# The second attention layer of a two-block network and its norm, put at the head of the scheduler's queue

## Chip, cores and metric

One Trainium2 chip, and of it one core. The metric is the time of one execution on the device in microseconds (us), as the median of several runs; lower is better. The profile is of one execution.

## What is computed

A first block of two layers works on 256 tokens of width 1024; a second block follows it. In the first block each layer is a norm, an attention with two families of heads, an output projection, a second norm and a gated feed-forward with a short causal convolution:

```python
for i in range(DEPTH):                       # DEPTH = 2, S = 256, D = 1024
    h = rms_norm(x, ln_attn_g[i])
    dq, dk, dv, mq, mk, mv = jnp.split(h @ w_in[i], cuts, axis=-1)   # 6 x 512 columns
    ...                                      # heads of dq, dk, mq, mk are normed
    y_diff = diff_attention(dq, dk, dv, lam, lam_init, diff_subln_g[i], bias_diff)
    y_moba = moba_attention(mq, mk, mv, bias_moba)
    x = x + jnp.concatenate([y_diff, y_moba], axis=-1) @ w_out[i]
    x = x + conv_ffn(rms_norm(x, ln_ffn_g[i]), w_up[i], conv_w[i], conv_b[i], w_down[i])
```

The second block takes this x (the "latent") and a second sequence of 256 tokens (the "context"). Its first layer runs a recurrence (rwkv7) over both, forwards and backwards: the context's end states are the start states of the latent's. The context's half of that needs nothing of the first block.

## The kernel before

Every product of activations and weights is made of three matrix products: `weights` (L256 to L270) loads a block of weights into a tile `raw` by a DMA on SP, rounds it into `whi` on ACT (L265), and puts the difference `raw - whi` into `wlo` on DVE or GpSimd (L269); `proj` (L276) and `feat_block` (L298) then issue three matmuls for each 128 rows. TensorE (PE) thus has dense stretches of matmuls wherever weights flow.

Three lanes of work share the engines, each with its own pools of tiles: the latent (`self.lat`), the context (`self.cx`) and a side lane (`self.sd`) with a few small tiles. The kernel is written in the order first norm, setup, `context1` (the context's part of the second block's first layer, with its recurrence in two groups of head pairs), first layer 0, feed-forward 0, `rest` (the modulation `ada` of layer 0), norm 1, first layer 1, `side` (`ada` of layer 1, and the tables of `setup_odd`), feed-forward 1, second block. No order is written out by hand: a list scheduler plays the program through with planned durations and, on each engine, takes among the instructions that are ready the one that was written first. What comes out is a fixed order on each engine's queue; on the chip each queue runs in that order. Tiles of one tag are given out in the order in which they are written, so an instruction that needs a tile waits for the tiles of that tag that are written ahead of it.

By that rule all of `context1` stands ahead of first layer 1 wherever both are ready, and `side` and feed-forward 1 stand behind it. In the profile first layer 1 runs from about 531 to 745 us: its norm (`norm_T`, L354, with `rstd`, L334), six projections of 512 columns (`prj`, L292 to L294), each of them but the two of values followed by a norm of heads (`head_norm`, L385: squares on ACT, sums L394 and some ten small operations on DVE, and the product `hn` at L401), transposes (`q_T`, `k_T`), four heads of `diff_att`, `diff_out` (L618, another `head_norm`), four pairs of `moba_att`, and the output projection `wo`. A projection holds two of the four PSUM banks of tag A until its `hn` is written. The context's lines are those of `rwkv_group` (from L1155 on: `low`, `kss`, `rsq`, `AR`, `BK`, `sc`, `G`, `bkt`, the solve on GpSimd at L1333 and L1335, and the chain of eight steps, L1363 to L1433); the matmuls of `ada` are L778. Feed-forward 1 is `g`, `up` and `acc`. After its last matmul the scheduler may issue the context's output projection (`co`, in `context2`).

What the change touches:

```python
        net.rest()
        act1=net.first_norm(1, x)
        net.first_layer(1, x, act1)
        net.side()
        net.conv_ffn(1, x)
```

Of the kernel before, what the change touches and what calls it, by code (L numbers as in the profile page):

```python
# [1762 lines left out]
def run(tc, I, out, colw, cstw, keep):  # L1763
    nc = tc.nc
    with ExitStack() as ctx:
        net = Net(tc, I)
        net.pools(ctx)
        net.setup(colw, cstw, keep)
        x = [net.keep([128, D], F32, name=f"x{t}") for t in range(2)]
        for t in range(2):  # L1770
            nc.sync.dma_start(x[t], I["x"][0, t * 128:(t + 1) * 128])
        act=net.first_norm(0, x)
        net.setup_first()
        net.setup_second()
        net.context1()
        net.first_layer(0, x, act)
        net.conv_ffn(0, x)
        net.rest()
        act1=net.first_norm(1, x)
        net.first_layer(1, x, act1)  # L1780
        net.side()
        net.conv_ffn(1, x)
        net.second_block(x)
        net.store_x(x, out[0])
# [38 lines left out]
```

## Time and profile before

| | us |
|---|---|
| median of three runs (2081.31 to 2081.9) | 2081.49 |
| the profiled execution, its own time | 2083.04 |
| its span, first to last instruction | 2081.2 |
| PE busy in the span | 1908.7 (92%) |
| DVE busy | 1369.1 (66%) |
| ACT busy | 1025.4 (49%) |
| GpSimd (POOL) busy | 928.4 (45%) |

Busy times are of engines, not of their queues: an instruction that waits leaves its engine idle, and all that is behind it in that queue waits with it. A row of the timeline has its start, its length, the engine, the line, the operation, the tile written and the tiles read, the shape and the count of merged instructions; in brackets stands the engine's idle time before it and what ended that.

### The profile page before, as it was taken

How to read it: one execution, taken by the hardware profiler on the slowest of the kernel's cores; microseconds unless marked ns; L12 is line 12 of the kernel's file. 1: busy time of each engine (PE TensorE's matmuls, PEld its weight loads, DVE VectorE, ACT ScalarE, POOL GpSimd, SP SyncE). 2: the span in 40 equal slices, each digit the busy share in tenths (PEclk: the TensorE clock that was granted, in tenths of full speed). 3: DMA queues.
4: the chain of work that ended last, by engine and by line, in shares of the span. 5: the costliest groups of instructions: out<-in, count | busy, mean ns of one | idle time of the engine just before them, and what ended most of it. 6: DMA issues, size and time to landing. Idle time of an engine off the chain costs nothing. (4 is left out here: it accounts for less than half of the span.)

```text
span 2081.2 us, 37712 instructions
## 1 busy us (share of the span) xinstructions
PE 1908.7 (92%) x14178; PEld 1592.7 (77%) x14178; DVE 1369.1 (66%) x2855; ACT 1025.4 (49%) x1990; POOL 928.4 (45%) x621
## 2 busy tenths in 40 slices
PE   6989999989998889999898888998699989998998
PEld 4567868888665458899797777887599977777997
DVE  5575378856687555786679878557764468656444
ACT  4455455545454435465456553334454454654443
POOL 3235544693232444544545355446255454113453
PEclk9999999999999999999999998899899999998999
DMA  9957455445455565664573334427465526234562
GB/s 341 310 173 232 153 181 167 151 141 169 131 185 178 190 199 168 198 218 152 163 219 103 102 110 150 127 71 235 158 204 177 178 100 220 78 105 154 181 200 73
DMA packets 270815, 351.08 MB, mean 169 GB/s; under 512 B 43150, under 2 KB 195469, under 8 KB 270632
## 3 DMA queue, kind: packets, MB, share of 16 engines
q1 hardware_dynamic: 267992, 343.32, 51.9%
q0 software_dynamic: 1968, 4.33, 0.7%
q8 instruction: 112, 1.84, 0.4%
q10 hardware_dynamic: 672, 1.02, 0.1%
q14 instruction: 71, 0.58, 0.1%
HBM read 334.04 MB, written 14.55 MB: 167 GB/s over the span
## 5 line engine op out<-in xcount | busy, mean ns | idle before, releaser
L269 POOL TENSOR_TENSOR wlo<-raw,whi 128x1024 fp32r<-128x1024 f32 (+2 forms) x408 | 781.7, 1931 | 982.2 <-ACT whi L265 809.2
L265 ACT ACTIVATE whi<-raw 128x1024 fp32r<-128x1024 f32 (+2 forms) x600 | 507.8, 882 | 142.8 <-issue 35.0
L269 DVE TENSOR_TENSOR wlo<-raw,whi 128x1024 fp32r<-128x1024 f32 x192 | 305.4, 1591 | 108.2 <-ACT whi L265 94.2
L308 PE MATMUL f<-ah,whi 128*128 128x256 f32 x768 | 225.8, 294 | 15.2 <-ACT whi L265 14.5
L310 PE MATMUL f<-ah,wlo 128*128 128x256 f32 x768 | 226.8, 295 | 7.6 <-POOL wlo L269 7.6
L309 PE MATMUL f<-al,whi 128*128 128x256 f32 x768 | 225.4, 294 | 0.5 <-DVE al L383 0.5
L746 PE MATMUL acc<-whi,hh 128*128 128x512 f32 x432 | 168.3, 393 | 2.1 <-ACT hh L461 2.1
L747 PE MATMUL acc<-wlo,hh 128*128 128x512 f32 x432 | 169.2, 392 | 0.0
L308 PEld LDWEIGHTS f<-ah,whi 128*128 128x128 f32 x768 | 153.6, 200 | 19.2 <-ACT whi L265 15.7
L748 PE MATMUL acc<-whi,hl 128*128 128x512 f32 x432 | 165.3, 391 | 0.4 <-DVE hl L462 0.4
L310 PEld LDWEIGHTS f<-ah,wlo 128*128 128x128 f32 x768 | 153.7, 200 | 11.7 <-POOL wlo L269 8.7
L309 PEld LDWEIGHTS f<-al,whi 128*128 128x128 f32 x768 | 153.8, 200 | 3.0 <-DVE al L383 0.9
L1584 DVE TENSOR_TENSOR r<-r 128x512 f32<-128x512 f32 x48 | 41.2, 858 | 129.4 <-ACT r L1583 128.3
L1583 ACT ACTIVATE r<-f 128x512 f32<-128x512 f32 x48 | 28.7, 598 | 179.2 <-PE f L310 179.0
L293 PE MATMUL prj<-wlo,ah 128*128 128x512 f32 (+1 forms) x272 | 108.2, 399 | 2.7 <-DVE wlo L269 1.6
L292 PE MATMUL prj<-whi,ah 128*128 128x512 f32 (+1 forms) x272 | 108.9, 406 | 0.4 <-DVE bt L499 0.4
L310 PE MATMUL g<-ah,wlo 128*128 128x256 f32 x352 | 102.1, 290 | 6.3 <-POOL wlo L269 6.3
L294 PE MATMUL prj<-whi,al 128*128 128x512 f32 (+1 forms) x272 | 106.2, 398 | 1.4 <-DVE al L383 1.4
L778 PE MATMUL ada<-adaw,kept 128*32 128x512 f32 x384 | 96.8, 636 | 8.6 <-DMA adaw<-in_w_ada_dram 8.3
L308 PE MATMUL g<-ah,whi 128*128 128x256 f32 x352 | 102.7, 292 | 0.4 <-DVE kept L786 0.4
L310 PE MATMUL up<-ah,wlo 128*128 128x256 f32 x352 | 101.4, 288 | 1.2 <-POOL wlo L269 1.2
L309 PE MATMUL g<-al,whi 128*128 128x256 f32 x352 | 102.3, 291 | 0.0
(473 smaller groups left out, 4861.2 us busy)
## 6 DMA issues: line engine op xcount, KB each, us to landing
raw<-in_w_ff_dram SPq DMA_DIRECT2D x128, 512.0 KB, 4.1
raw<-in_w_up_dram SPq DMA_DIRECT2D x88, 512.0 KB, 4.6
adaw<-in_w_ada_dram SPq DMA_DIRECT2D x144, 256.0 KB, 5.0
raw<-in_w_ff_dram SPq DMA_DIRECT2D x128, 256.0 KB, 3.9
raw<-in_w_in_dram SPq DMA_DIRECT2D x48, 512.0 KB, 4.7
raw<-in_w_down_dram SPq DMA_DIRECT2D x44, 512.0 KB, 4.1
adaw<-in_w_ada_dram SPq DMA_DIRECT2D x24, 512.0 KB, 7.3
raw<-in_w_out_dram SPq DMA_DIRECT2D x24, 512.0 KB, 4.4
```

Of the source, the lines that this page charges most:

```text
L265: nc.scalar.activation(hi, raw, AF.Copy)
L269: eng.tensor_tensor(lo, raw, hi.bitcast(F32), op=OP.subtract)
L292: nc.tensor.matmul(ps[t][:, :n], ah, wh[:, k], start=st, stop=False)
L293: nc.tensor.matmul(ps[t][:, :n], ah, wl[:, k], start=False, stop=False)
L294: self.last = nc.tensor.matmul(ps[t][:, :n], al, wh[:, k], start=False, stop=en)
L308: nc.tensor.matmul(pv[:, j], wh[:, k % a, c], ah, start=first, stop=False, skip_group_check=skip)
L309: nc.tensor.matmul(pv[:, j], wh[:, k % a, c], al, start=False, stop=False, skip_group_check=skip)
L310: nc.tensor.matmul(pv[:, j], wl[:, k % a, c], ah, start=False, stop=k == 7, skip_group_check=skip)
L746: nc.tensor.matmul(acc[t][n], hh[:, k, c], wh[:, n], start=st, stop=False)
L747: nc.tensor.matmul(acc[t][n], hh[:, k, c], wl[:, n], start=False, stop=False)
L748: self.last = nc.tensor.matmul(acc[t][n], hl[:, k, c], wh[:, n], start=False, stop=en)
L778: nc.tensor.matmul(ps[32 * j:32 * j + 32], self.sT[:, k], raw[:, k - kb], start=k < 4, stop=k >= 4)
```

## The change

A context manager of the scheduler is put around two calls. The instructions traced inside are numbered from the start of the program instead of by their place in it, so that in the scheduler's choice among ready instructions they stand ahead of everything that is written after the first few hundred instructions: of `context1`'s recurrence, of feed-forward 0 and of `rest`. Dependencies, tiles, counts of buffers and the instructions themselves stay.

```diff
         net.rest()
-        act1=net.first_norm(1, x)
-        net.first_layer(1, x, act1)
+        with tc.high_priority():
+            act1=net.first_norm(1, x)
+            net.first_layer(1, x, act1)
         net.side()
```

## Rows read from the trace of the kernel before

**Rows 1.** The page, part 1: busy us and share of span, each engine.

```profile
PE 1908.7 (92%) x14178; PEld 1592.7 (77%) x14178; DVE 1369.1 (66%) x2855; ACT 1025.4 (49%) x1990; POOL 928.4 (45%) x621
```

**Rows 2.** Windows: length, busy us (PE, PEld, DVE, ACT, POOL), clock, DMA share, GB/s.

```profile
500.00:540.00 40.00, 36.20 (x410) 30.10 (x408) 28.12 (x60) 21.46 (x45) 14.94 (x7) 0.99 0.34 101
...
600.00:660.00 60.00, 50.91 (x287) 33.68 (x286) 50.42 (x155) 27.10 (x61) 11.47 (x5) 0.94 0.50 165
660.00:700.00 40.00, 32.72 (x244) 20.21 (x242) 28.82 (x96) 20.62 (x57) 9.30 (x14) 0.91 0.79 249
...
740.00:760.00 20.00, 13.77 (x63) 6.16 (x61) 11.87 (x31) 8.70 (x18) 9.66 (x13) 0.83 0.71 221
760.00:880.00 120.00, 120.00 (x1300) 98.05 (x1299) 75.73 (x177) 55.08 (x105) 46.11 (x41) 1.00 0.61 183
880.00:985.00 105.00, 103.27 (x729) 97.20 (x728) 79.31 (x105) 60.85 (x82) 49.09 (x23) 1.00 0.62 193
```

**Rows 3.** Windows of tile adaw alone: length, busy us of PE and PEld.

```profile
360.00:530.00 170.00, 0.00 (x0) 0.00 (x0) 0.97 0.49 150
```

**Rows 4.** Timeline of PE: idle places in and ahead of first layer 1.

```profile
540.63 0.69 PE L1373 MATMUL P<-uv,G 32*64 32x64 f32 x8 [0.90 <-PE P L1378]
...
638.60 0.66 PE L784 MATMUL adaT<-kept,asb 128*128 128x128 f32 x4 [1.95 <-ACT asb L780]
642.59 5.05 PE L778 MATMUL ada<-adaw,kept 128*32 128x512 f32 x12 [3.33 <-DMA adaw<-in_w_ada_dram]
...
687.37 0.66 PE L1315 MATMUL bkt<-kept,ic 128*128 128x128 f32 x4 [1.12 <-DVE ic L1311]
...
691.06 0.45 PE L1373 MATMUL P<-uv,G 32*64 32x64 f32 x8 [1.61 <-DMA nm<-G]
...
693.94 1.33 PE L624 MATMUL oT<-kept,hn 128*128 128x128 f32 x5 [2.05 <-DVE hn L401]
```

**Rows 5.** Timeline of DVE: the norm of the second family's keys.

```profile
637.30 1.25 DVE L394 TENSOR_REDUCE hst<-sq 128x8 f32<-128x512 f32 x2
...
641.89 0.69 DVE L1217 TENSOR_TENSOR kn<-kn,sq 128x512 f32<-128x512 f32 x1 [1.05 <-DMA sq<-rs]
...
649.50 1.29 DVE L401 TENSOR_TENSOR hn<-prj,rsq_y 128x512 f32<-128x512 f32 x2
```

**Rows 6.** Timeline of DVE: the norm of the first family's keys.

```profile
583.01 0.69 DVE L394 TENSOR_REDUCE hst<-sq 128x8 f32<-128x512 f32 x1
...
587.15 1.29 DVE L401 TENSOR_TENSOR hn<-prj,rsq_y 128x512 f32<-128x512 f32 x2
```

**Rows 7.** Timeline of DVE: the norm in diff_out.

```profile
683.13 1.26 DVE L394 TENSOR_REDUCE hst<-sq 128x4 f32<-128x512 f32 x2
...
693.19 1.29 DVE L401 TENSOR_TENSOR hn<-od,rsq_y 128x512 f32<-128x512 f32 x2
```

**Rows 8.** Timeline of DVE: context instructions inside the norm ahead of layer 1.

```profile
538.18 1.13 DVE L1422 TENSOR_TENSOR kept<-P,kept 64x128 f32<-64x128 f32 x4
539.33 1.20 DVE L1433 TENSOR_TENSOR Y<-P,Y 32x128 f32<-32x128 f32 x4
```

**Rows 9.** Waits of PE, 600 to 700 us: total, times, longest.

```profile
PE ada L778 <- DMA adaw<-in_w_ada_dram: 5.8, 4, 3.3
```

**Rows 10.** Groups of DVE by line, 600 to 700 us: busy, mean ns.

```profile
L1210 DVE SCALAR_TENSOR_TENSOR lw<-lw 128x64 f32<-128x64 f32 x14 | 3.5, 274 | 0.1
...
L250 DVE TENSOR_SCALAR rs<-q 4x256 int32<-4x256 int32 x1 | 0.3, 275 | 0.0
```

**Rows 11.** Timelines: the context recurrence's last DVE row; the first matmul of co.

```profile
897.28 0.42 DVE L1457 TENSOR_TENSOR z<-yT,z 128x256 f32<-128x256 f32 x1
...
997.99 0.39 PE L292 MATMUL co<-whi,yh 128*128 128x512 f32 x1
```

**Rows 12.** Timelines of DVE and POOL at the same moment.

```profile
630.59 2.60 DVE L254 SCALAR_TENSOR_TENSOR rs<-q,rs 4x256 f32<-4x256 f32 x1
...
630.50 2.42 POOL L269 TENSOR_TENSOR wlo<-raw,whi 128x1024 fp32r<-128x1024 f32 x1 [16.90 <-ACT whi L265]
```

## The prediction

> **What bounds the kernel now.** The first view is the page's account of busy time: PE works 1908.7 of 2081.2 us, every other engine at most 66% [rows 1]. The change takes no matmul away, so it can only win back idle time of PE: all of it is 172.5 us. The second view, the windows, says where that idle time lies near the change. First layer 1 runs from about 541 to 745 us; PE idles 9.09 us in 600 to 660, 7.28 us in 660 to 700 and 6.23 us in 740 to 760, the norm that follows it [rows 2]. From 760 to 880 it does not idle at all, and from 880 to 985, the rest of feed-forward 1, only 1.73 us [rows 2]. So the stretch is worth at most 22.6 us, 16.4 of them inside the layer, and whatever work is pushed out of the layer into feed-forward 1 takes there exactly its own PE time: nothing is free there, but nothing is lost either.
>
> The third view tells what else runs in 600 to 700: DVE is busy 50.42 of 60 us and 28.82 of 40 [rows 2], so DVE is the fuller engine beside PE, and a third of it is not the layer's. The context's recurrence has 32 groups of DVE there, from 3.5 us (L1210) down to 0.3 us (L250) [rows 10], together about 39 us. The fourth view, the timeline of PE, shows gaps of which the releaser is seldom the layer itself: PE stands in front of `ada` or context matmuls [rows 4], because the layer has nothing ready. What it lacks is read on DVE.
>
> **What the change does to the order.** The layer's instructions win over the context's wherever both are ready, on all five queues. They do not start earlier than their tiles and data allow. That tiles are given out in the order of writing is seen from `adaw`: the side lane's `ada` of layer 1 needs only weights, yet from 360 to 530 us not one such matmul runs [rows 3]; it waits until norm 1, written ahead of it, has taken its tiles. So I exclude that the layer's weights crowd out those of feed-forward 0, and nothing before about 500 us should move.
>
> **The terms.** I look for the places where context instructions lie between dependent instructions of the layer while PE idles.
> (a) The norm of heads of the first keys, nearly undisturbed, takes from the end of its second sum (583.01 + 0.69 = 583.70) to its product at 587.15: 3.45 us [rows 6]. The same norm of the second keys takes from 637.30 + 1.25 = 638.55 to 649.50: 10.95 us [rows 5]. Between stand the context's products of 0.69 us and less, the first of them at 641.89 [rows 5]. Difference 7.50 us. The projection of the values behind it needs the PSUM banks that these keys hold, so PE has only `ada`: it idles 1.95 + 3.33 = 5.28 us [rows 4].
> (b) The norm in `diff_out` takes from 683.13 + 1.26 = 684.39 to 693.19: 8.80 us [rows 7], 5.35 more than the undisturbed one; PE idles 1.12 + 1.61 + 2.05 = 4.78 us [rows 4].
> (c) In norm 1 eight context instructions, 1.13 + 1.20 = 2.33 us, stand inside the chain of the first rstd [rows 8]; PE idles 0.90 us just behind them [rows 4].
> The layer so gets shorter by at least 7.50 + 5.35 + 2.33 = 15.2 us, and the idle time in these places is 5.28 + 4.78 + 0.90 = 10.96 us. The 15.2 us are not the gain: the context's and the side lane's matmuls which filled the difference come later, into feed-forward 1, at their own price [rows 2]. The gain is the idle time that goes.
> What comes back: between the layer's own latencies PE still has to live on `ada`, which waits for its DMAs 5.8 us in this stretch [rows 9]; 3.33 of these are counted in (a) [rows 4], the other 2.5 I expect to be met once more, because a shorter layer calls for the same weights sooner. Net: 10.96 - 2.5 = 8.5 us. Bounds: below, nothing is won, or some us are lost, if other waits take these places; above, all the idle time of 600 to 700 goes, and (c): 16.4 + 0.9 = 17.3 us.
>
> Edits at nothing. On SP the layer's loads of `w_in` and `w_out` go ahead of the context's `uv` and `feat` and of `adaw`; what hides that delay is the context's slack: its last DVE instruction is at 897.28, and its first consumer, `co`, starts at 997.99, behind the last matmul of feed-forward 1 [rows 11]. The context can slip by 100 us before anyone waits; past that each us would be lost on the context's side alone, beside dense work of the latent. On ACT, DVE and POOL the roundings of the layer's first weights can go ahead of feed-forward 0's last operations; PE idles there 3.8 of 40 us [rows 2]; I take 0, with 3.8 us either way as the bound (a gain there is possible for the same reason as in (c)). On POOL the context's solve, some 60 small products, comes later by as much as the context does; it has POOL nearly for itself. The `side` lane and feed-forward 1 stood behind the layer before and still do.
>
> **Sum.** The profiled execution took 2083.04 us for a span of 2081.2; 2083.0 - 8.5 = 2074.5. It stands 1.5 us above the median of the runs, so for the median 2081.5 - 8.5 = 2073.0.
>
> **A rule that speaks against it.** DVE's product at L254 on 4x256 elements took 2.60 us at 630.59, while POOL's `wlo` ran from 630.50 to 632.92 [rows 12]: one engine held the other up. The Trainium skill, GPSIMD Engine Reference, section Specifications, says the same in general: the SBUF interfaces of GpSimd are shared with VectorE, and it names DVE instructions with two SBUF inputs as those that contend. By that rule, more POOL and DVE work in the same stretch costs more than its sum. The solve and the context's preparation would move from a stretch with little `wlo` on POOL into feed-forward 1 with much of it; it is the second rival, whose price below comes from busy times alone.
>
> **The rivals.**
> 1. *The idle time only moves.* The layer is shorter, but PE then waits in it for weights of `ada`, and in feed-forward 1's norm, in full. For it: `ada` is what PE does between the layer's steps, and its waits are for DMAs [rows 9], with the DMA engines 0.79 busy in 660 to 700 [rows 2]. Against it: the context's own matmuls are then a backlog that can fill. It gives 2081.5, give or take 4. The same time comes if the scheduler, whose planned durations are not the chip's, finds the context and the layer ready at other moments and hardly changes their order.
> 2. *DVE becomes the bound in feed-forward 1.* If the layer runs through first, the context's preparation comes after it, and there it stands ahead of feed-forward 1. Feed-forward 1 without the context keeps DVE busy 79.31 of 105 us, 0.755 [rows 2]. The preparation's stretch was about 87 us long, from 600 to its transposes `bkt` at 687 [rows 4]; its 39 us of DVE [rows 10] beside the feed-forward's 0.755 x 87 = 65.7 make 104.7 us in 87: PE would miss 17.7 us of work. Less the 8.5 won: 9.2 us slower, 2090.7. It decides from the point on at which the context's preparation (`low`, `kss`, `AR`, `BK`) begins behind the layer's last `wo`. Against it: the preparation needs only the end of the first group's chain, which is well under way when the layer starts [rows 4, 8], and the layer's own latencies leave DVE room, 9.6 us in 600 to 660 and 11.2 in 660 to 700 [rows 2]; and beside the context's chain DVE was busy only 75.73 of 120 [rows 2].
> 3. *All the idle time in the layer goes*: 17.3 us, 2064.2; I count it as the far end of my case.
>
> **How the numbers follow.** The forecast, faster by 4 to 20 us, has 0.52; rival 1 has 0.26; rival 2, and any other loss from a newly made order, 0.22. A measurement of this kernel can tell about 0.2%, 4.2 us, from no change. Faster 0.52, the same 0.26, slower 0.22. The forecast's own range is 2062 to 2077. Eight times in ten the time should lie between 2061, a little past the far end of my case, and 2092, just past the price of rival 2: I leave out a tenth on either side, because a new order is made for the whole rest of the kernel and its stalls aren't in any row.
>
> **What would show it.** Right: before 500 us the timeline is as it was; the norms of heads in first layer 1 take 3 to 5 us each; `wo` ends 15 us or more earlier; PE's idle time in 600 to the end of `wo` falls to about half; the context's last `z` comes later than 897 but ahead of `co`; the last matmul of feed-forward 1 comes 5 to 15 us before 998; from there on both traces run alike, shifted. Rival 1 shows as an earlier `wo` with an unmoved `co`, and larger waits for `adaw`. Rival 2 shows as idle PE in feed-forward 1 with DVE over 0.9 busy. I am wrong altogether if first layer 1 is not shorter, if something ahead of 500 us moves, or if the difference arises behind 1000 us.

## The result, and the profile of the changed kernel

The changed kernel takes 2114.64 us (median of 4, 2110.86 to 2116.84), the kernel before 2081.47 us (median of 4): a ratio of 1.0149, 95% interval 1.0130 to 1.0168. The forecast was 2073.0 us, 8 us faster; it is 33 us slower, beyond the range. The profiled execution of after took 2112.45 us for a span of 2110.7, 29.5 us more than the span of before.

Where the time goes is read first on PE's share. Page of after, part 1, busy us and share of the span:

```profile
PE 1927.8 (91%) x14178; PEld 1600.6 (76%) x14178; DVE 1367.9 (65%) x2855; ACT 1025.1 (49%) x1990; POOL 931.6 (44%) x621
```

The same 14178 matmuls as in [rows 1], but 19.1 us more busy time: matmuls have become slower, and the idle time has grown by 10.4 us (182.9 for 172.5). The windows say where. They are cut at the last matmul of feed-forward 0, the last of `wo` and the first of `co`; so the first row is norm 1 with first layer 1, the second feed-forward 1 with its norm; the columns are those of [rows 2]. Kernel before:

```profile
533.40:742.80 209.40, 186.78 (x1222) 126.57 (x1225) 150.24 (x437) 96.73 (x218) 76.77 (x75) 0.94 0.54 175
742.80:998.00 255.20, 245.13 (x2121) 207.70 (x2120) 174.23 (x320) 128.74 (x209) 105.78 (x76) 0.99 0.60 184
```

Changed kernel:

```profile
533.00:745.20 212.20, 193.50 (x1148) 126.57 (x1151) 143.53 (x423) 94.75 (x212) 46.20 (x24) 0.93 0.52 173
745.20:1026.90 281.70, 261.26 (x2195) 220.06 (x2196) 190.81 (x333) 129.39 (x216) 139.01 (x126) 0.94 0.53 168
```

The layer is not shorter but 2.8 us longer; feed-forward 1 is 26.5 us longer; up to 533 us and behind the first `co` (1083.2 and 1083.8 us to the end) the lengths have changed by no more than 0.6 us. In feed-forward 1 PE idles 281.70 - 261.26 = 20.4 us instead of 10.1, and its mean granted clock is 0.94 instead of 0.99. The clock has two levels, 2.4 and 1.2 GHz, so a mean of 0.94 over 281.7 us is about 2 x 0.06 x 281.7 = 34 us at the lower one; before it was 6.8 us. PE worked in 30.0 of these 34.1 us, and in 4.9 of the 6.8. What a microsecond of work at the lower clock costs is shown further down: 0.44 us.

How far the context has slipped, in rows of after (PE, then DVE, then PE; the solve's first and last product on POOL). Answering rows of before are [rows 11] and, for the solve, 696.05 to 750.34:

```profile
613.32 0.69 PE L1378 MATMUL P<-kept,AR 64*64 64x64 f32 x8
665.11 1.13 PE L1172 MATMUL low<-tz,kept 128*128 128x512 f32 x2
745.12 0.91 PE L1294 MATMUL sc<-AR,BK 64*64 64x64 f32 x42
...
760.41 0.23 POOL L1333 TENSOR_TENSOR Ttmp<-T 64x30 f32<-64x30 f32 x1
836.87 0.26 POOL L1335 TENSOR_TENSOR T<-T,Ttmp 64x30 f32<-64x30 f32 x1
...
983.80 0.42 DVE L1457 TENSOR_TENSOR z<-yT,z 128x256 f32<-128x256 f32 x1
1026.86 0.39 PE L292 MATMUL co<-whi,yh 128*128 128x512 f32 x1
```

The end of the first group's chain (L1378) has slipped from 579 to 614 us, the second group's preparation (`low` to `sc`) from 615 to 682 us to 665 to 746, the solve by 64 us, the last `z` by 86.5. All this is inside the 100 us that the prediction gave the context: `z` is 43 us ahead of `co`.

**The layer.** The norm of the second family's keys, DVE, answering [rows 5]; the end of the second sum is 633.37 + 0.66 = 634.03:

```profile
633.37 0.66 DVE L394 TENSOR_REDUCE hst<-sq 128x8 f32<-128x512 f32 x1
...
637.43 0.17 DVE L252 TENSOR_TENSOR rsq_t<-rsq_y 128x16 f32<-128x16 f32 x1
637.64 0.79 DVE L1422 TENSOR_TENSOR kept<-P,kept 64x128 f32<-64x128 f32 x3
...
642.91 1.28 DVE L401 TENSOR_TENSOR hn<-prj,rsq_y 128x512 f32<-128x512 f32 x2
...
677.29 1.25 DVE L394 TENSOR_REDUCE hst<-sq 128x4 f32<-128x512 f32 x2
684.33 1.29 DVE L401 TENSOR_TENSOR hn<-od,rsq_y 128x512 f32<-128x512 f32 x2
```

It takes 642.91 - 634.03 = 8.88 us; before it took 10.95. Between its dependent steps of 0.17 us there still stand context rows: now the steps of the first group's chain (L1400, L1422, L1433). The norm in `diff_out` takes 684.33 - 678.54 = 5.79 us (8.80 before [rows 7]); there the preparation, which has moved into the attention, stands between. Both norms together are 5.1 us shorter, and at the end of the second the layer is 8.5 us ahead: 151.3 us from its start, 159.8 before. What is left of the layer, the four pairs of `moba_att` and `wo`, before and then after:

```profile
693.20:742.80 49.60, 47.06 (x214) 31.22 (x218) 24.40 (x68) 20.52 (x50) 37.77 (x56) 0.94 0.52 167
684.30:745.20 60.90, 58.22 (x326) 36.37 (x330) 35.05 (x100) 25.02 (x62) 10.93 (x7) 0.97 0.56 181
```

Here 11.3 us are lost, not by idle time (2.5 and 2.7 us) but by work: 112 matmuls more, 90 of them `sc`, 8 `bkt` and 10 others of the preparation, and 4 `ada`. In the kernel before all these matmuls of the preparation ran ahead of the end of that norm. So the layer won its 8.5 us and paid them back, because the preparation came late but did not leave the layer.

**Feed-forward 1.** All places where PE idles over 0.6 us in that stage, before and then after. Before:

```profile
744.54 0.66 PE L784 MATMUL adaT<-kept,asb 128*128 128x128 f32 x4 [0.80 <-ACT asb L780]
749.58 0.44 PE L370 MATMUL nT<-kept,xn 128*128 128x128 f32 x2 [3.39 <-DVE xn L362]
753.35 1.54 PE L370 MATMUL nT<-kept,xn 128*128 128x128 f32 x6 [1.94 <-DVE xn L362]
892.01 0.44 PE L1452 MATMUL yT<-kept,Y 128*128 128x128 f32 x2 [1.73 <-DVE Y L1447]
991.72 0.50 PE L746 MATMUL acc<-whi,hh 128*128 128x512 f32 x1 [1.72 <-ACT hh L461]
```

After, and behind them the windows in which these places lie:

```profile
750.97 0.63 PE L1315 MATMUL bkt<-kept,ic 128*128 128x128 f32 x4 [2.39 <-DVE ic L1311]
752.88 0.41 PE L370 MATMUL nT<-kept,xn 128*128 128x128 f32 x2 [0.74 <-DVE xn L362]
754.94 2.54 PE L778 MATMUL ada<-adaw,kept 128*32 128x512 f32 x4 [1.65 <-DMA adaw<-in_w_ada_dram]
769.87 0.66 PE L784 MATMUL adaT<-kept,asb 128*128 128x128 f32 x4 [0.75 <-ACT asb L780]
831.63 1.04 PE L1097 MATMUL cb<-fl,chk 128*64 128x128 f32 x12 [2.93 <-DMA chk<-rpb_line]
873.42 0.41 PE L1407 MATMUL P<-uv,G 32*32 32x64 f32 x8 [0.64 <-DVE uv L1400]
875.72 0.45 PE L1373 MATMUL P<-uv,G 32*64 32x64 f32 x8 [1.50 <-ACT Y L1431]
912.74 0.41 PE L1394 MATMUL P<-xs,TT 32*32 32x64 f32 x8 [1.27 <-DVE xs L1388]
977.73 0.44 PE L1452 MATMUL yT<-kept,Y 128*128 128x128 f32 x2 [2.31 <-DVE Y L1447]
1004.24 0.39 PE L310 MATMUL up<-ah,wlo 128*128 128x256 f32 x1 [0.75 <-POOL wlo L269]
1019.44 0.79 PE L746 MATMUL acc<-whi,hh 128*128 128x512 f32 x1 [5.39 <-ACT hh L461]
```
```profile
750.00:770.00 20.00, 15.89 (x81) 6.97 (x82) 10.35 (x35) 8.66 (x21) 8.18 (x21) 0.74 0.78 248
830.00:836.00 6.00, 4.37 (x22) 3.54 (x23) 2.31 (x5) 1.23 (x3) 5.59 (x8) 0.72 0.99 319
873.00:888.00 15.00, 13.08 (x130) 11.24 (x130) 6.72 (x19) 4.19 (x11) 5.22 (x5) 0.66 0.55 153
977.00:983.00 6.00, 5.27 (x29) 5.06 (x30) 5.63 (x9) 1.85 (x4) 1.80 (x2) 0.72 0.00 0
1016.00:1024.00 8.00, 4.56 (x12) 3.63 (x13) 3.28 (x4) 0.63 (x1) 2.11 (x1) 0.57 0.41 131
```

These five windows are 2 x (0.26 x 20 + 0.28 x 6 + 0.34 x 15 + 0.28 x 6 + 0.43 x 8) = 34 us at the lower clock: all that the stage has. So most of these stalls are paid twice, first as idle time and then as a stretch of slower matmuls; behind those of 1.27 us at 912.74 and 0.75 us at 1004.24 the clock stayed at 1.00. By places, idle time and 0.44 of the work of PE at the lower clock, against before:

| place | before | after | more |
|---|---|---|---|
| the norm, with `bkt` and `ada` (745 to 770) | 6.1 + 2.1 | 5.5 + 4.0 | 1.3 |
| the tables `cb`, waiting for a DMA | 0 | 2.9 + 1.5 | 4.4 |
| the second group's chain, then its `yT` | 1.7 | 5.7 + 6.0 | 10.0 |
| the last unit (`wlo`, then `acc`) | 1.7 | 6.1 + 1.7 | 6.1 |

Together 21.8 of the 26.5 us; the rest is not traced to places, but the stage has 74 matmuls more (2195 for 2121). In the last unit PE does not wait for a step of the chain. On DVE the product `hl` (2.56 us) and a `wlo` of 3.43 us stand ahead of the last unit's `cg`, which so runs at 1008.01, though its matmuls were done at 1001.8 and its step on ACT at 1004.50:

```profile
1002.18 2.56 DVE L462 TENSOR_TENSOR hl<-cu,hh 128x512 fp32r<-128x512 f32 x1 [0.24 <-ACT hh L461]
1004.66 3.43 DVE L269 TENSOR_TENSOR wlo<-raw,whi 128x1024 fp32r<-128x1024 f32 x1
1008.01 0.47 DVE L700 SCALAR_TENSOR_TENSOR cg<-g,kept,cg 128x255 f32<-128x255 f32 x1
```

Yet the slip of the context reaches this place, too. Its result is read back (`yr`) and split for `co` (`yh` on ACT, `yl` on DVE). Before, `yh` ran at 905.16 and 910.98, far from the last unit. Now it runs at 995.35 and 999.62, just ahead of that unit's steps on ACT, and ACT idles 4.15 and 1.81 us in front of it:

```profile
999.62 1.06 ACT L461 ACTIVATE yh<-yr 128x1024 fp32r<-128x1024 f32 x1 [1.81 <-DMA yr<-ctxy]
```

No run moved this split alone, so its part of the 6.1 us is not shown.

### The profile page after: what moved, and what is told of

It reads as the page before. It is cut to its first block, busy times and chain, and to the rows that moved or that the text cites. A ratio compares the mean times of both kernels' runs of the same rounds, so it can differ in the third digit from the quotient of the medians.

```text
span 2110.7 us, 37690 instructions
## 1 busy us (share of the span) xinstructions
PE 1927.8 (91%) x14178; PEld 1600.6 (76%) x14178; DVE 1367.9 (65%) x2855; ACT 1025.1 (49%) x1990; POOL 931.6 (44%) x621
## 5 line engine op out<-in xcount | busy, mean ns | idle before, releaser
L269 DVE TENSOR_TENSOR wlo<-raw,whi 128x1024 fp32r<-128x1024 f32 x192 | 318.0, 1656 | 125.9 <-ACT whi L265 112.7
L778 PE MATMUL ada<-adaw,kept 128*32 128x512 f32 x384 | 103.0, 642 | 8.5 <-DMA adaw<-in_w_ada_dram 8.2
```

Of the source, the lines that this page charges most:

```text
L269: eng.tensor_tensor(lo, raw, hi.bitcast(F32), op=OP.subtract)
L778: nc.tensor.matmul(ps[32 * j:32 * j + 32], self.sT[:, k], raw[:, k - kb], start=k < 4, stop=k >= 4)
```

## The experiments

Theory A: the loss comes with the slip of the context's second group, whose chain falls late into feed-forward 1. Theory B: it is that group's solve on GpSimd beside the feed-forward's `wlo`. Theory C: any newly made order costs, whatever slips. Executions of the kernel before spread from 2076 to 2097 us on the chips of these runs, so each kernel is judged by its ratio to executions of before on the same chip. All in one table (lengths from one trace each, cut as above; idle time of PE and mean granted clock in feed-forward 1; end of the last `z`):

| kernel | ratio (95%) | layer 1 | feed-forward 1 | idle, clock | `z` |
|---|---|---|---|---|---|
| before | 1 | 209.4 | 255.2 | 10.1, 0.99 | 897.7 |
| before_again | one execution | 210.6 | 255.3 | 10.1, 0.99 | 897.4 |
| after | 1.0149 (1.0130 to 1.0168) | 212.2 | 281.7 | 20.4, 0.94 | 984.2 |
| after_again | 1.0147 (1.0111 to 1.0182) | 212.2 | 281.6 | 21.5, 0.94 | 985.7 |
| norm_only | 1.0098 (1.0083 to 1.0113) | 216.8 | 260.8 | 12.8, 0.97 | 909.6 |
| layer_only | 1.0132 (1.0113 to 1.0152) | 213.5 | 267.7 | 11.0, 0.98 | 999.2 |
| heads_only | 0.9996 (0.9978 to 1.0013) | 209.2 | 255.6 | 12.0, 0.97 | 898.3 |
| nochain_before | 0.9873 (0.9831 to 0.9915) | 213.3 | 224.3 | 6.4, 0.98 | |
| nochain_after | 0.9922 (0.9898 to 0.9946) | 212.2 | 237.2 | 10.8, 0.96 | |
| from_step4 | 1.0110 (1.0066 to 1.0155) | 219.6 | 260.0 | 12.3, 0.96 | 896.4 |
| g2_behind_layer | 1.0031 (1.0009 to 1.0053) | 205.6 | 267.4 | 12.7, 0.98 | 914.8 |
| g2_at_wo | 1.0147 (1.0124 to 1.0169) | 191.1 | 277.8, to its last `acc` | 20.0, 0.96 | 1041.7 |
| chain2_free | 1.0002 (0.9988 to 1.0015) | 210.6 | 255.2 | 9.9, 0.99 | 895.6 |
| chain2_unit3 | 1.0060 (1.0036 to 1.0085) | 211.1 | 260.5 | 13.5, 0.97 | 990.2 |
| solve2_at_wo | 1.0046 (1.0032 to 1.0060) | 209.1 | 254.5 | 11.1, 0.98 | 907.4 |
| solve2_held | 1.0062 (1.0043 to 1.0081) | 207.2 | 265.1 | 13.0, 0.96 | 970.4 |
| after_side_held | 1.0330 (1.0307 to 1.0352) | 198.6 | 311.9 | 19.1, 0.95 | 973.9 |
| wo_only | 1.0019 (1.0004 to 1.0034) | 213.0 | 254.6 | 10.7, 0.97 | 901.4 |
| tables_only | 1.0023 (1.0007 to 1.0039) | 209.4 | 255.4 | 9.1, 0.98 | 911.3 |

One thing bears on several rows. In norm_only, layer_only, g2_at_wo, solve2_at_wo, solve2_held and tables_only the queues of PE, DVE, ACT and GpSimd hold another order than in before already ahead of 100 us, hundreds of microseconds ahead of the lines that were edited; it is one and the same in all six, and after_side_held has a third. In the other kernels these four queues are as in before up to 500 us. Feed-forward 0 ends at 536.3 to 539.2 us in the six (537.8 on average), at 530.1 to 538.2 where the order is that of before (533.4 on average). So some 4 us of the totals of these six, 0.2%, need not come from what their edit is about. Why the scheduler plans them so is open. The changed kernel itself has the order of before there.

**Yardsticks.** The two kernels unchanged.

> The kernel before once more, as a yardstick for the other traces of this series: how far the lengths of the stages (to the end of feed-forward 0, first layer 1, feed-forward 1, and so on) differ between two executions of one program. Expected: each stage within 5 us of the first trace (533, 209, 255, 446, 238, 399 us).

> The changed kernel once more, as a yardstick: its stages beside those of its first trace (first layer 1 212 us, feed-forward 1 282 us). If the 26 us in feed-forward 1 belong to the order of the queues, they are there again, within 5 us; if they are a chance of one execution, feed-forward 1 is back at 255 to 265 us.

Both stages come out within 1.2 us of the first traces, and the stalls of feed-forward 1 return: 2.51 us at `bkt`, 2.90 at `cb`, 1.50 and 1.25 in the chain, 2.31 at `yT`, 5.38 in the last unit. The time at the lower clock is 34.1 us again, though not behind the same stalls: none follows the one at `yT`, and 17 us instead of 10 lie in the norm. So the 26.5 us belong to the order of the queues, not to one execution.

**The parts of the change, each alone.**

```diff
-        act1=net.first_norm(1, x)
+        with tc.high_priority():                # norm_only
+            act1=net.first_norm(1, x)
```
```diff
-        net.first_layer(1, x, act1)
+        with tc.high_priority():                # layer_only
+            net.first_layer(1, x, act1)
```

> Only the norm ahead of the layer (norm 1) gets the priority, step (c) of the prediction by itself. By the rows it is worth 0.9 us of idle PE; it can push the last steps of the first group's chain back by some us only. Theory A: slip under 15 us, so 2078 to 2090 us. Theory C: 2090 to 2115 us.

> Only first layer 1 gets the priority, its norm does not: the other part of the change alone. Theory A: the second group slips as in the changed kernel, so the loss is there in full: 2105 to 2120 us, feed-forward 1 275 to 285 us. If the norm's part were what matters: 2081 to 2090 us.

Either part alone loses most of the whole (2108.8 and 2110.9 us). The expectation for norm_only by theory A is wrong: `z` slips by 12 us only, and its loss is spread, 7.4 us in the layer, 5.6 in feed-forward 1, 4.7 ahead of them, where its order is another as said above, the rest behind. In layer_only `z` slips by 101 us, more than in the changed kernel (86.5), but feed-forward 1 has only 12.5 us more. So the slip doesn't set the loss. layer_only also shows that shorter norms are not yet a shorter layer: the two of (a) and (b) take 6.34 and 4.92 us there, 8.5 less than before, and the layer is 4.1 us longer.

**Steps (a) and (b) by themselves.** `head_norm` of layer 1 is called inside the priority; its projections are not.

```diff
-            on = self.head_norm(L, [o[:, t] for t in range(2)], 4, 128)
+            on = self.raised(i, [o[:, t] for t in range(2)], 4, 128)   # head_norm under high_priority if i
```

> Only the five norms of heads of first layer 1 (two of queries, two of keys, one in diff_out) get the priority, nothing else. It is steps (a) and (b) of the prediction by themselves. If these steps are right and free: the layer's stage gets shorter by up to 10 us (the 5.28 and 4.78 us of idle PE), the context's second group slips by the 10 us of DVE that it gives up at most, so theory A (the loss comes with that group's slip) sees no loss in feed-forward 1: 2071 to 2082 us. Theory C (any newly made order loses some 10 to 30 us): 2090 to 2110 us.

No gain, no loss. Its DVE rows show context work between the norm's steps as before:

```profile
639.35 1.25 DVE L394 TENSOR_REDUCE hst<-sq 128x8 f32<-128x512 f32 x2
643.16 0.69 DVE L1217 TENSOR_TENSOR kn<-kn,sq 128x512 f32<-128x512 f32 x1 [0.28 <-DMA sq<-rs]
...
650.37 1.29 DVE L401 TENSOR_TENSOR hn<-prj,rsq_y 128x512 f32<-128x512 f32 x2
```

From the end of the second sum at 640.60 to the product the norm takes 9.77 us, 10.95 before; the one in `diff_out` takes 7.74 (8.80). The likely reason is that the raised instructions are not ready when the context's are, as each waits for the one ahead of it; the scheduler's plan is in no trace, so that is argued from the order alone. The "if these steps are right and free" of the expectation could not happen by this means.

**Without the chain.** The same edit in both kernels:

```diff
-        for i in range(8):
+        for i in range(0 if s and p0 else 8):
```

> The kernel before without the eight steps of the chain (L1363 to L1433) of the context's second group; its preparation and its solve on GpSimd stay. Left out of the computation: these eight steps (their result Y is set to a constant). In the trace of before the chain's matmuls take 136 us of PE between 740 and 885. Both theories: some 100 to 136 us less than before, 1945 to 1981 us; the pair's difference decides, see the next kernel.

> The changed kernel without the same eight steps (left out of the computation in the same way). Theory A: the 33 us are lost because this chain comes some 87 us later and falls one step after the other into the part of feed-forward 1 that had been dense, where the steps' small matmuls keep PE waiting in its queue and are followed by stretches at half the clock. Then without the chain in both kernels the difference is gone: 0 to 8 us above the kernel without the chain made from before. Theory B: the solve of the second group (60 products on GpSimd), now inside feed-forward 1, is what costs, or the layer itself; it is still there, so at least 20 of the 33 us remain.

Removing the chain from before saves 26 us (ratio 0.9873), not 100 as expected by every theory: the 136 us are summed busy times of small matmuls that overlap others, and no price; in the trace of before the steps from 691 to 874 us cover only 24.6 us of PE's time. (The last `z` of these kernels says nothing and is left out.)

In feed-forward 1 the difference without the chain is 12.9 us (237.2 and 224.3), with it 26.5: 13.6 us need the chain's presence, near the 10.0 read at its places above, and half of the loss does not. The whole difference falls from 1.0149 to 0.9922 / 0.9873 = 1.005.

**Doses of slip.** from_step4 ranks the layer just ahead of the fifth step of the first group's chain instead of at the start; the other two write the second group behind the layer (`net.group2()`), free or held to the last `wo`:

```diff
+        with tc.high_priority(offset=tc.tile_snap_priority() - net.group_at):   # from_step4
+            act1=net.first_norm(1, x)
+            net.first_layer(1, x, act1)
```
```diff
         net.first_layer(1, x, act1)
+        net.group2()                      # g2_behind_layer
+        net.behind([net.group2])          # g2_at_wo: issued behind self.last
```

> The layer and its norm stand ahead of the fifth step of the first group's chain in the queue, not ahead of everything: they pass only the last four steps. Theory A: the chain of the first group ends less late, the second group slips less than 87 us, and the loss is about in proportion to the slip (33 us for 87): between 2085 and 2105 us. Theory C (any newly made order costs, whatever slips): no relation of the loss to the slip; it may be 2110 with a small slip or 2081 with a large one.

> The context's second group written behind first layer 1 (ahead of the side lane), and no priority: the layer passes the second group's preparation, solve and chain, but not the first group's chain. Theory A: the first group's chain ends as before (579 us), the second group's preparation slips by some 20 to 50 us, and the loss is a part of the 33 us: 2085 to 2105 us. If it is the first group's chain tail alone that matters: 2080 to 2085 us. Theory C: no relation to the slip.

> The context's second group (preparation, solve and chain) is held back until the last matmul of the layer's output projection has been issued; nothing is raised. Theory A: the layer's stage gets shorter than 209 us by 5 to 15 us, since the preparation is out of it; the second group's last z comes 100 us later than in the kernel before or more (after 1000 us), feed-forward 1 takes 30 to 60 us longer than its 255 us, and the total is 2095 to 2135 us: the largest slip has the largest loss in feed-forward 1. If the loss does not hang on the slip, feed-forward 1 takes no more than the 282 us that it takes in the changed kernel.

from_step4 speaks for C against A: no slip at all of `z`, and 23 us lost, 10 in the layer, 5 in feed-forward 1; another 5 are there by 538 us, in an order that is still that of before. g2_at_wo shows what the layer is worth with the preparation quite out of it, and where that comes back:

```profile
536.70:727.80 191.10, 175.32 (x1024) 117.52 (x1024) 118.29 (x354) 87.37 (x188) 46.71 (x22) 0.95 0.56 187
```

The layer takes 18.3 us less than before, the size that the prediction gave it (15.2 or more), and feed-forward 1 takes 22.6 us more, up to its own last matmul; the chain's end at 1041.7 then holds up `co`. The norms show it directly. From the end of the second sum (636.51 + 0.68 = 637.19) the norm of the second keys takes 4.52 us, and the one in `diff_out` 2.58:

```profile
636.51 0.68 DVE L394 TENSOR_REDUCE hst<-sq 128x8 f32<-128x512 f32 x1
...
641.71 0.69 DVE L401 TENSOR_TENSOR hn<-prj,rsq_y 128x512 f32<-128x512 f32 x1
```

That is 6.43 and 6.22 us less than before, 12.65 in all, where (a) and (b) of the prediction add up to 12.85.

**Only the chain late, then solve and chain late.** The second group's chain is written behind feed-forward 1 and given its old rank; with or without one wait:

```diff
+        with tc.high_priority(offset=tc.tile_snap_priority() - net.chain2_at):   # chain2_free
+            net.chain2()                  # chain2_unit3: also inside tc.issue_after(net.unit[3].ins)
```

> The kernel before with the chain of the context's second group written behind feed-forward 1 but given back its old place in the queue; a control for the next kernel, with which it is the same but for one wait. Expected by every theory: as the kernel before, 2081 to 2090 us, feed-forward 1 (last wo to the first co) 255 us.

> The same, and the chain of the second group is held until the last matmul of the fourth of the eleven units of feed-forward 1 has been issued. Layer 1, the preparation and the solve stay as they were before: only the chain is late, by some 60 to 90 us, about as much as in the changed kernel. Theory A (a late chain costs by itself): feed-forward 1 takes 265 to 285 us, the total is 10 to 30 us above the control. Rival (the loss is made in the layer, by the preparation or by the solve on GpSimd): feed-forward 1 within 5 us of 255, the total within 5 us of the control.

The control is as before. With `z` 92.5 us late, more than in the changed kernel, feed-forward 1 takes 5.3 us longer: half of the 10 us that theory A asks at the least. (The total is 12.6 us above the control's; 4.4 of that are there by 534 us, and what else lies outside feed-forward 1 is in small pieces.)

For the solve there are two kernels. solve2_at_wo orders it behind `wo` in the plan only; solve2_held lets GpSimd first copy one column of the x that the last `wo` writes:

```diff
         tmp = L.mid([np_, 256], name="Ttmp")
+        self.held is None or nc.gpsimd.tensor_copy(tmp[:, 0:1], self.held[0:np_, 1023:1024])   # solve2_held
```

> Nothing is raised; the solve of the context's second group (60 products on GpSimd) is held until the last matmul of the layer's output projection, and the chain behind it comes late with it. Preparation and layer stay. Theory B (the solve beside the feed-forward's wlo on GpSimd costs, on top of the 5 us of a late chain): feed-forward 1 takes 275 to 285 us, the total is 15 to 35 us above before. If neither the solve nor the chain is what costs: feed-forward 1 at most 262 us, and the loss of the changed kernel hangs on what the preparation and the first group's last steps do in the layer, or on no single cause.

> The solve of the second group now really held: its first product on GpSimd waits, by data, for the layer's last sum into x, so it starts at about 746 us instead of 696 (760 in the changed kernel), and the chain behind it about 50 us or more late. In solve2_at_wo the solve had run at 705 to 756 us all the same, so that kernel told nothing of it. The preparation stays in the layer. Theory B (the solve beside feed-forward 1): feed-forward 1 takes 270 to 285 us instead of 255, total 2100 to 2115 us. Rival (the preparation that falls out of the layer is what costs; solve and chain late alone are dear only by the 5 us of chain2_unit3): feed-forward 1 255 to 263 us, total 2080 to 2095 us.

solve2_at_wo missed its aim: GpSimd reached the solve at 704.86 all the same, since nothing but the planned order held it. In solve2_held it starts at 749.04:

```profile
749.04 0.23 POOL L1336 TENSOR_TENSOR Ttmp<-T 64x30 f32<-64x30 f32 x1
824.19 0.28 POOL L1338 TENSOR_TENSOR T<-T,Ttmp 64x30 f32<-64x30 f32 x1
```

The solve takes 75.4 us beside the feed-forward's `wlo`, as in the changed kernel (76.7), instead of 54.3, and `z` is 73 us late; yet feed-forward 1 takes 9.9 us more. Solve and chain late together are worth some 10 of the 26.5 us, the solve about half of that by the difference to chain2_unit3. Theory B, by which feed-forward 1 should have taken 270 to 285 us, falls.

**Is it the cover?** The side lane of the changed kernel, held until the chain begins:

```diff
+        with tc.issue_after(net.begun.ins):
-        net.side()
+            net.side()
```

> The changed kernel, with the side lane (the modulation of layer 1 and the tables of setup_odd) held until the first step of the second group's chain. In the kernel before, these independent matmuls ran beside the chain's first steps; in the changed kernel they ran while the solve was still under way and were used up when the chain came. If what the late chain lacks is such cover, feed-forward 1 takes less than its 282 us, 255 to 268, and the total is 2085 to 2100 us. If the chain is just as dear with cover, or the cover is missed as much where it is taken from: 2110 us or more.

69 us slower than before: PE idles 39.6 us in the layer, where `ada` had filled the waits, and all of `ada` comes on top of feed-forward 1. The cover is missed as much where it is taken from; whether the chain became cheaper beside it can't be told from this.

**Small new orders.**

```diff
+            with self.tc.high_priority() if i else nullcontext(): self.proj(...)         # wo_only
+        with self.tc.high_priority(): [None for _ in self.setup_odd(self.sd)]             # tables_only
```

> Only the output projection of first layer 1 (its last some 125 instructions of 955) is raised: a small new order from about 715 us on, and the context's second group slips by a few us at most. Theory A and B: no loss, 2079 to 2088 us. Theory C (no single cause: every newly made order puts PE's queue behind other waits, and each stall can be paid again at the lower clock): 2086 to 2110 us, in stages that the edit does not touch.

> Only the side lane's tables (setup_odd: eight small steps with some ten matmuls each) are raised; layer 1, its norm and the context's order against each other stay as they were. Theory A and B: no loss, 2079 to 2088 us, since the context's second group does not slip. Theory C: 2086 to 2110 us.

Both leave feed-forward 1 at 254.6 and 255.4 us, and lose about 0.2%; in tables_only, with the other order, 5.8 us are late already at the end of feed-forward 0. So theory C, in its plain form, falls too: a new order as such does not make feed-forward 1 longer.

None of the kernels that do the whole computation is faster than the kernel before.

**What stands.** With only the chain late feed-forward 1 loses 5.3 us; with solve and chain late 9.9; with preparation, solve and chain late and nothing raised 22.6; in the changed kernel 26.5. So some 10 us go with the late solve and chain, and the larger part comes when the preparation, too, comes late. These are differences between single traces, and solve2_held and g2_at_wo have the other order ahead. And layer_only, with a larger slip, loses 12.5 there and the rest elsewhere. Which entries of the new order put `cb`, the chain's steps and the last unit's `cg` behind their waits was read from the trace, and no run changed these entries alone. Nor is it settled why norm_only and from_step4 lose some 20 us in small pieces over all stages; PE's queue behind `co`, too, holds another order in them than in before.

## Why the prediction was wrong

- **The layer shorter by at least 15.2 us**: it got 2.8 us longer. This step failed in two ways. The first is the place to which the displaced work goes. It was to "come later, into feed-forward 1"; 108 matmuls of the preparation came behind the norm in `diff_out` instead, still inside the layer, and the 8.5 us that had been won up to there were lost again in the 11.3 us that the rest of the layer took longer.
- **The terms**: (a) was to give 7.50 us and gave 10.95 - 8.88 = 2.07; (b) 5.35, and gave 8.80 - 5.79 = 3.01; (c) gave nothing that the first `prj` shows (547.7 and 547.5 us). This is the second way: "the layer's instructions win over the context's wherever both are ready" does not keep a chain of dependent 0.17 us steps free of context rows. heads_only shows that by itself; that the next step isn't ready while the last one runs is the likely reason. Nor was all of (a) the context's: rows of the layer itself, which no priority of the whole layer moves, stand in the same 10.95 us, the longest of them

```profile
638.47 2.36 DVE L596 TENSOR_SCALAR L<-L,r 128x128 f32<-128x128 f32 x2
```

- **The size of these terms was right, its condition not met**: with the preparation held out of the layer (a) and (b) give 12.65 of 12.85 us, and the layer is 18.3 us shorter (g2_at_wo).
- **Work pushed into feed-forward 1 "takes there exactly its own PE time: nothing is free there, but nothing is lost either"**: this is the step that lost the 26.5 us. Of them 10.4 are new stalls of PE and some 11 the lower clock; the other 5 are not traced. A stretch without idle time was taken for one without waits; the likely reading is that before, the waits were met by other ready work that stood next in PE's queue, and that the new order has other work there.
- **"The context can slip by 100 us before anyone waits"**: it slipped 86.5 us, and its consumer `co` did not wait for it, as forecast. But PE executes the context's own steps in its fixed order, and waits in front of them (0.64, 1.50, 1.27 and 2.31 us); and the split of its result for `co` fell into the last unit, where ACT waited for it 4.15 and 1.81 us. Slack at the end of a chain says nothing of that.
- **Rival 1** (idle time only moves) gave no change and an earlier `wo`; neither came, though PE's idle time in the layer did fall, from 22.6 to 18.7 us (21.4 and 20.8 in before_again and after_again). **Rival 2** had the sign and the place, by another mechanism: its condition, the preparation beginning behind the last `wo`, was not met (`low` at 665.11), and DVE was busy 190.81 of 281.7 us, 0.68, not over 0.9. Its chance, 0.22, was too small, and its 9.2 us too few, because new stalls and the slower clock behind them were no term of its sum.
- **The rule on shared ports** that the prediction weighed (the Trainium skill, GPSIMD Engine Reference, Specifications): the trace agrees that the solve takes longer beside `wlo`, 76.7 us for 54.3, but in the same queue `wlo` also stands between its products, so the ports' part isn't separated; and the whole is worth some 5 us of feed-forward 1.
- **A slip of reckoning**: the context's 39 us of DVE in 600 to 700 are half of the 79.24 us there, not a third. No term uses the third.
- **Nothing ahead of 500 us moved**: right. What stands behind `co` took as long as before (1083.8 and 1083.2 us), as forecast.

## What to carry to other kernels

A priority among ready instructions does not keep the gaps of a dependent chain free, and what it displaces is not gone: look at where the displaced work lands, and what PE will find next in its queue there. A stretch in which PE never idles is not free room but a balance of many waits and fillers; price work that is moved into it at its own time, and look in a stretch that already mixes such work for the idle time and the slower clock that come with it. Slack measured at a lane's end says nothing about the stalls that its steps, and the first steps of its consumer, cause in a shared in-order queue. And before two variants are compared stage by stage, see whether their queues agree where the edit has no business: six of these kernels differed from 30 us on.

## What the runs showed of the hardware

Stalls of PE much shorter than the stretch at half clock can stand ahead of it: around and behind 0.64 and 1.50 us of idle time near 875 us the clock was 0.66 on average over 15 us, that is 10 us at 1.2 GHz. And the same stall is not always followed by it. Ahead of layer 1 PE's queue holds the same matmuls in the same order in the kernel before and in from_step4; both stall at the same place, and only in one does the clock fall (PE, before, then from_step4):

```profile
177.97 1.26 PE L624 MATMUL oT<-kept,hn 128*128 128x128 f32 x8 [2.67 <-DVE hn L401]
...
179.63 0.28 PE L310 MATMUL sh<-ah,wlo 128*128 128x256 f32 x1
179.75 0.28 PE L308 MATMUL sh<-ah,whi 128*128 128x256 f32 x1
```
```profile
178.42 1.57 PE L624 MATMUL oT<-kept,hn 128*128 128x128 f32 x8 [2.65 <-DVE hn L401]
...
180.34 0.41 PE L310 MATMUL sh<-ah,wlo 128*128 128x256 f32 x1
180.55 0.41 PE L308 MATMUL sh<-ah,whi 128*128 128x256 f32 x1
```

A matmul of 256 columns starts every 0.12 us at 2.4 GHz and every 0.21 us at 1.2 GHz, so a microsecond at the lower clock does 0.56 of the work: 0.44 us is lost, the factor used above. The Trainium skill (TensorE: Matmul & The Clock Gate, HAM oscillation) books one half of the time at the lower clock as lost; the trace nearly agrees. By 538 us from_step4 is 4.9 us late, ahead of anything that it changes, with 4.3 us more idle time of PE and 27.3 instead of 20.5 us at the lower clock; how much of the one brought the other is not shown. This puts a floor under what one trace can tell about a few microseconds.
